# Add and RMS norm on one core: loops run to the last but one tile, and GpSimd itself waits for the last stores

## The chip, the cores and the metric

The kernel runs on one core of a Trainium2 chip. The metric is the device time of one execution in microseconds (us). The spread of the kernel before over several chips and sessions was 3725.68 to 3726.74 us. The engines are named as in the profile: DVE is VectorE, ACT is ScalarE, POOL is GpSimd, SP is SyncE; a trailing q (SPq, DVEq) marks the engine's sequencer, under which the traces list waits, branches, register operations and DMA issues.

## The reference

```python
batch, seq, dim = 32, 2048, 2048          # float32; gamma is all ones, eps 1e-6
z = x + residual
rms = np.sqrt(np.mean(z ** 2, axis=-1, keepdims=True) + eps)
return (z / rms * gamma).astype(np.float32)
```

There are 65,536 rows of 8 KB. Two inputs are read and one output is written once, 1610.7 MB in all.

## The kernel before

Each of the 128 partitions takes up to seven rows at a time, so a full tile is 128 x 7 x 2048 floats. There are 74 tiles, 0 to 73 (`last` is 73). SyncE issues every transfer. VectorE adds the residual, ScalarE squares and sums and takes the root, VectorE inverts and scales. Two z buffers alternate. The last tile comes in four pieces and has code of its own.

```python
last = n_tiles - 1                       # 73
LO = 3
n_iter = (last - 1 - LO) // 2            # 34
HI = LO + 2 * n_iter                     # 71
...
def sp_turn(sp, t):
    i = t.i
    t.wait(sp, "done", -1)               # the tile before is scaled
    # store of tile i - 1
    ...
    t.wait(sp, "add_a")
    load_r(sp, t, 1)                     # residual of tile i + 1
    t.wait(sp, "s_out", -1)              # the store has landed: its z is free
    # load of x of tile i + 1 (in four pieces where that is the last)
...
def sync_program(sp):
    ...
    for i in range(1, n_tiles):
        sp_turn(sp, Turn(i))
    for k, (a, b) in enumerate(tail):    # (0,2), (2,4), (4,6), (6,7)
        sp.wait_ge(tail_ev["done"], k + 1)
        sp.dma_start(out=rows(o_f, last)[:, a:b, :], in_=z[last % 2][:, a:b, :]
                     ).then_inc(s_tail, U)
    sp.wait_ge(s_tail, U * len(tail))
    sp.wait_ge(ev["s_out"][(last - 1) % 2], ((last - 1) // 2 + 1) * U)
    sp.sem_inc(fin, 1)
...
def vector_program(v):                   # scalar_program has the same shape
    ...
    for i in range(LO):
        dve_turn(v, Turn(i), lambda i, h: (2 * i + h + 1) * U)
    with v.Fori(0, 2 * n_iter, 2) as it:
        for i in range(LO, LO + 2):
            dve_turn(v, Turn(i, it), lambda i, h: it * (2 * U) + (2 * i + h + 1) * U)
    for i in range(HI, last):            # tiles 71 and 72, written out
        dve_turn(v, Turn(i), lambda i, h: (2 * i + h + 1) * U)
    # ... the last tile
...
nc.gpsimd.wait_ge(fin, 1)
nc.gpsimd.sem_clear(range(ids[0], ids[-1] + 1))
```

Inside a loop the threshold of each wait depends on the pass and is computed in a register (476 register operations on ScalarE's L209 in the trace of before, 14 in each of 34 passes); in a written-out turn it is a constant.

Of the kernel before, what the change touches and what calls it, by code (L numbers as in the profile page):

```python
# [9 lines left out]
def kernel(  # L10
# [17 lines left out]
    nc = tc.nc  # L28
# [12 lines left out]
    U = 16  # L41
# [8 lines left out]
    last = n_tiles - 1  # L50

    LO = 3
    n_iter = (last - 1 - LO) // 2
    HI = LO + 2 * n_iter
    assert n_iter >= 1

    def rows(t, i):
        k = sizes[i]
        return t[starts[i] : starts[i] + P * k, :].rearrange("(p r) m -> p r m", r=k)
# [11 lines left out]
    def sem(name):  # L71
        sems.append(ctx.enter_context(nc.semaphore(name)))
        return sems[-1]
# [17 lines left out]
    ev = {k: [sem(f"{k}{p}") for p in range(2)] for k in names}  # L91
# [4 lines left out]
    s_tail = sem("s_tail")  # L96
    fin = sem("fin")
# [3 lines left out]
    tail = [(0, 2), (2, 4), (4, 6), (6, 7)]  # L101
# [30 lines left out]
    def load_x(sp, t, d=0):  # L132
        i = t.i + d
        inc(sp.dma_start(out=z[i % 2][:, : sizes[i], :], in_=rows(x_f, i)), "x_in", i)

    def load_r(sp, t, d=0):
        i = t.i + d
        e = entry(i)
        inc(
            sp.dma_start(out=r_area[:, e : e + sizes[i], :], in_=rows(r_f, i)),  # L140
            "r_in",
            i,
        )

    def sp_turn(sp, t):
        i = t.i
        t.wait(sp, "done", -1)
        inc(
            sp.dma_start(out=rows(o_f, i - 1), in_=z[(i - 1) % 2][:, : sizes[i - 1], :]),
            "s_out",  # L150
            i - 1,
        )
        if i == last:
            return
        t.wait(sp, "add_a")
        load_r(sp, t, 1)
        t.wait(sp, "s_out", -1)
        if i + 1 == last:
            for k, (a, b) in enumerate(tail):
                sp.dma_start(  # L160
                    out=z[last % 2][:, a:b, :], in_=rows(x_f, last)[:, a:b, :]
                ).then_inc(x_tail[k], U)
        else:
            load_x(sp, t, 1)
# [84 lines left out]
    def sync_program(sp):  # L249
        load_x(sp, Turn(0))  # L250
        load_r(sp, Turn(0))

        sp.wait_ge(tail_ev["add"], 1)
        for q in range(4):
            sp.dma_start(  # L255
                out=stage[32 * q : 32 * q + 1],
                in_=gamma.partition_broadcast(1).rearrange("p (a b) -> p a b", a=16),
            ).then_inc(g_in, U)
        load_r(sp, Turn(1))
        load_x(sp, Turn(1))  # L260
        for i in range(1, n_tiles):
            sp_turn(sp, Turn(i))
        for k, (a, b) in enumerate(tail):
            sp.wait_ge(tail_ev["done"], k + 1)
            sp.dma_start(
                out=rows(o_f, last)[:, a:b, :], in_=z[last % 2][:, a:b, :]
            ).then_inc(s_tail, U)
        sp.wait_ge(s_tail, U * len(tail))
        sp.wait_ge(ev["s_out"][(last - 1) % 2], ((last - 1) // 2 + 1) * U)
        sp.sem_inc(fin, 1)  # L270

    def vector_program(v):
        v.memset(eps_tile[:, :], float(eps))  # L273
# [28 lines left out]
    def scalar_program(s):  # L302
# [13 lines left out]
        for k, (a, b) in enumerate(tail):  # L316
# [4 lines left out]
            ).then_inc(tail_ev["rms"], 1)  # L321

    sync_program(nc.sync)
    vector_program(nc.vector)
    scalar_program(nc.scalar)


    nc.gpsimd.wait_ge(fin, 1)
    ids = [a.num for a in sems]
    assert ids == list(range(ids[0], ids[0] + len(ids)))  # L330
    nc.gpsimd.sem_clear(range(ids[0], ids[-1] + 1))
# [35 lines left out]
```

## Time and profile before

| what | value |
|---|---|
| time, median of the first three runs | 3726.35 us (3725.92 to 3726.7) |
| span of the profiled run | 3724.7 us |
| VectorE, ScalarE busy | 62%, 29% |
| DMA share in each of 40 slices, and rate | 90% or more; mean 432 GB/s, steady 434 |
| instruction packets in the span | 4 |

The prediction below shows the lines of the page and of the waits. Two views that it only tells in words are these. The first is the list of DMA issues (transfer, engine, count, KB each, median us from issue to landing); the second the instructions of two lines at the end (count, shortest/median/longest duration in ns, first and last start in us):

```profile
out_dram<-z SPq DMA_DIRECT2D x71, 7168.0 KB, 34.5
```

```profile
L270 SPq EVENT_SEMAPHORE  x1: 28/28/28, 3723.5 to 3723.5; - x1
```

```profile
L331 POOLq EVENT_SEMAPHORE_RANGE_CLEAR  x1: 185/185/185, 3723.6 to 3723.6; - x1
```

A transfer is counted as landed when the last of its semaphore updates has arrived. A store takes 34.5 us to land with other transfers in flight: 7.34 MB alone at 434 GB/s would be 16.9 us (an estimate). The four instruction packets are of 8,192 bytes each in the trace, on a DMA queue of their own (q14); a packet is read here as a block of an engine's program, and is called a page of code below. And the end is a chain of very short things: SyncE sees the last store landed, tells GpSimd, and GpSimd clears the semaphores.

### The profile page before, as it was taken

What the parts mean: (1) busy time and instruction counts of PE and PEld (TensorE: products, weight loads), DVE (VectorE), ACT (ScalarE), POOL (GpSimd) and SP (SyncE); (2) the same over time, 40 slices, a digit from 0 to 9 for tenths busy, and PEclk for the clock granted to TensorE, in tenths of its full rate; (3) what the DMA queues carried; (4) which work ended last, traced back from release to release, by engine and by line L of the source; (5) the groups of instructions that cost most, each with busy time, mean ns of one, the idle gap of its engine ahead of it and who ended that gap; (6) DMA issues with size and microseconds to landing.
All of it is one profiled execution on the core that took longest, in us unless ns stands there. A gap on an engine that the chain in (4) does not pass through costs nothing.

```text
span 3724.7 us, 3652 instructions
## 1 busy us (share of the span) xinstructions
DVE 2302.5 (62%) x816; ACT 1072.4 (29%) x1176; POOL 0.2 (0%) x4
## 2 busy tenths in 40 slices
DVE  5666665566665566665566665566665566655566
ACT  2233322233322233322233322233322233322233
POOL 0000000000000000000000000000000000000000
DMA  9999999999999999999999999999999999999999
GB/s 420 432 434 434 434 434 434 432 434 434 435 434 434 434 434 436 434 434 434 433 434 434 434 434 434 434 434 434 434 434 434 434 434 434 434 434 434 434 434 398
DMA packets 32964, 1610.69 MB, mean 432 GB/s; under 512 B 3712, under 2 KB 3776, under 8 KB 3776
## 3 DMA queue, kind: packets, MB, share of 16 engines
q1 hardware_dynamic: 32960, 1610.66, 99.9%
q14 instruction: 4, 0.03, 0.0%
HBM read 1073.77 MB, written 536.87 MB: 432 GB/s over the span
## 4 chain that ended last, share of the span: by engine, by line
DMA 66%; DVE 22%; issue 9%; ACT 2%; SPq 0%; DVEq 0%; ACTq 0%
DMA out_dram<-z 33%; DMA z<-in_x_dram 33%; DVE z L170 15%; DVE z L175 7%; ACT sq_junk L221 1%; DMA r_area<-in_gamma_dram 0%; ACT rms L229 0%; DVE rstd L195 0%; DVEq L126 0%; SPq L255 0%; DVE r_area L274 0%; ACTq L209 0%; ACTq L126 0%; DVE tail_rstd L291 0%; SPq L160 0%
## 5 line engine op out<-in xcount | busy, mean ns | idle before, releaser
L170 DVE TENSOR_TENSOR z<-z,r_area 128x8192 f32<-128x8192 f32 (+2 forms) x150 | 1109.4, 7437 | 1253.2 <-DMA z<-in_x_dram 1227.6
L221 ACT ACTIVATE sq_junk<-z 128x2048 f32<-128x2048 f32 x512 | 963.4, 1882 | 2618.1 <-DVE z L170 2606.7
L175 DVE SCALAR_TENSOR_TENSOR z<-z,rstd,gamma_tile 128x2048 f32<-128x2048 f32 x505 | 1153.5, 2344 | 5.2
L195 DVE RECIPROCAL rstd<-rms 128x4 f32<-128x4 f32 (+2 forms) x146 | 25.3, 173 | 130.8 <-ACT rms L229 130.8
L221 ACT ACTIVATION_READ_ACCUMULATOR sq_junk<-z 128x1 f32 x512 | 95.4, 186 | 0.0
L229 ACT ACTIVATE rms<-ssq,eps_tile 128x4 f32<-128x4 f32 (+2 forms) x146 | 43.3, 297 | 13.4
L175 DVE SCALAR_TENSOR_TENSOR z<-z,tail_rstd,gamma_tile 128x2048 f32<-128x2048 f32 x7 | 16.2, 2346 | 0.1
L276 DVE LOAD_MASK_SELECT gamma_tile<-r_area x1 | 0.0, 14 | 16.4 <-DMA r_area<-in_gamma_dram 16.4
L276 DVE STREAM_SHUFFLE gamma_tile<-r_area 128x2048 f32<-128x2048 f32 x1 | 2.3, 2290 | 0.0
L274 DVE MEMSET r_area<- 128x2048 f32 x1 | 1.8, 1765 | 0.4 <-issue 0.4
L221 ACT ACT_TABLE_LOAD x1 | 1.3, 1283 | 0.9 <-SPq L75 0.9
L229 ACT ACT_TABLE_LOAD x1 | 1.3, 1283 | 0.1
L229 ACT ACTIVATE tail_rms<-tail_ssq,eps_tile 128x2 f32<-128x2 f32 (+1 forms) x4 | 1.2, 296 | 0.1
L273 DVE MEMSET eps_tile<- 128x1 f32 x1 | 0.1, 59 | 1.0 <-SPq L75 1.0
L291 DVE RECIPROCAL tail_rstd<-tail_rms 128x2 f32<-128x2 f32 (+1 forms) x4 | 0.6, 158 | 0.0
L348 POOL MEMSET const-bfloat16-1.0<- 128x1 bf16 x1 | 0.1, 102 | 0.0
L348 POOL MEMSET const-uint8-127<- 128x1 uint8 x1 | 0.1, 102 | 0.0
L348 POOL MEMSET const-float32-1.0<- 128x1 f32 x1 | 0.1, 99 | 0.0
L348 POOL MEMSET const-float32-0.0<- 128x1 f32 x1 | 0.1, 98 | 0.2 <-issue 0.2
## 6 DMA issues: line engine op xcount, KB each, us to landing
r_area<-in_residual_dram SPq DMA_DIRECT2D x72, 7168.0 KB, 27.2
z<-in_x_dram SPq DMA_DIRECT2D x71, 7168.0 KB, 33.8
out_dram<-z SPq DMA_DIRECT2D x71, 7168.0 KB, 34.5
z<-in_x_dram SPq DMA_DIRECT2D x3, 2048.0 KB, 26.3
out_dram<-z SPq DMA_DIRECT2D x3, 2048.0 KB, 13.9
r_area<-in_residual_dram SPq DMA_DIRECT2D x1, 5120.0 KB, 25.3
z<-in_x_dram SPq DMA_DIRECT2D x1, 5120.0 KB, 36.8
out_dram<-z SPq DMA_DIRECT2D x1, 5120.0 KB, 24.7
```

The costliest lines, as they stand in the source:

```text
L170: return v.tensor_add(out=s, in0=s, in1=r_area[:, e + a : e + b, :])
L175: ins = v.scalar_tensor_tensor(out=s, in0=s, scalar=rs[:, c + g - a : c + g - a + 1], in1=gamma_tile[:, :], op0=mult, op1=mult,)
L195: v.reciprocal(out=rstd[p][h][:, :n], in_=rms[p][h][:, :n]).then_inc(dve, U)
L221: s.activation(out=sq_junk[:, :], in_=src[:, g, :], func=Act.Square, accum_out=sq[:, g - a : g - a + 1],)
L229: return s.activation(out=rm, in_=sq[:, : b - a], func=Act.Sqrt, bias=eps_tile[:, :], scale=inv_d)
L273: v.memset(eps_tile[:, :], float(eps))
L274: v.memset(stage, 0.0).then_inc(tail_ev["add"], 1)
L276: v.stream_shuffle(gamma_tile[:, :].rearrange("p (a b) -> p a b", a=16), stage, [0] * 32)
L291: v.reciprocal(out=tail_rstd[:, a:b], in_=tail_rms[:, a:b]).then_inc(dve, U)
L348: nc = _bacc.Bacc("TRN2", target_bir_lowering=False, num_devices=1)
```

## The change

The intent is less code and one handshake less. Both loops go on to tile 72, so no written-out turn is left between loop and last tile; and GpSimd, which only has to know that all stores have landed, waits for their semaphores itself.

```diff
-    n_iter = (last - 1 - LO) // 2
+    n_iter = (last - LO) // 2
@@ sync_program
-        sp.wait_ge(s_tail, U * len(tail))
-        sp.wait_ge(ev["s_out"][(last - 1) % 2], ((last - 1) // 2 + 1) * U)
-        sp.sem_inc(fin, 1)
@@ end
-    nc.gpsimd.wait_ge(fin, 1)
+    nc.gpsimd.wait_ge(ev["s_out"][(last - 1) % 2], ((last - 1) // 2 + 1) * U)
+    nc.gpsimd.wait_ge(s_tail, U * len(tail))
```

## The prediction

> **What bounds the kernel now.** I read the page first, then the chain of waits in order of time, then the instructions in order of time round the last loop pass and the end. From the page:
>
> ```profile
> span 3724.7 us, 3652 instructions
> ...
> DVE 2302.5 (62%) x816; ACT 1072.4 (29%) x1176; POOL 0.2 (0%) x4
> ...
> DMA  9999999999999999999999999999999999999999
> ...
> DMA packets 32964, 1610.69 MB, mean 432 GB/s; under 512 B 3712, under 2 KB 3776, under 8 KB 3776
> ...
> DMA 66%; DVE 22%; issue 9%; ACT 2%; SPq 0%; DVEq 0%; ACTq 0%
> ```
>
> VectorE (DVE) is busy 62% of the span and ScalarE (ACT) 29%, while the DMA engines are at 90% or more in each of the forty slices. The work is two inputs and one output of 536.87 MB, 1610.69 MB in all; at the page's steady 434 GB/s that is 3711 us of a 3724.7 us span. So transfers bound it, and about 14 us is start and drain.
>
> The last row seems to say otherwise: the chain that ended last is a third compute. In order of time a full period of that chain reads: store 34.5 us, load of x 33.8, add 15.2, the wait for ScalarE 8.6, the scaling 9.1, and the next store: about 101.6 us for two tiles, because each of the two z buffers goes round once in two tiles. But two full tiles also move 6 transfers of 128 x 7 x 2048 x 4 bytes = 7.34 MB, which is 44.04 MB, and at 434 GB/s that is 101.5 us. The two agree since a landing time is stretched by the other transfers in flight; while the DMA row stays at 9, a shorter compute leg would be met by longer landings. The chain names the path, the DMA row the limit.
>
> [...] the trace has 50 to 69 ns for VectorE's loop branch and 40 to 50 ns for ScalarE's, so I use these. [...] The page of this trace has four instruction packets in the whole span (0.03 MB), and the DMA view from 3310 us to the end lists the data queue alone, although both loops leave at about 3561 us: here leaving the loop fetched nothing. [...]
>
> **The change, part by part.** There are 74 tiles, numbered 0 to 73. The loops start at tile 3 and take two tiles a pass.
>
> (1) The number of passes was (73 - 1 - 3) // 2 = 34, to tile 70, with tiles 71 and 72 written out after the loop; the trace has 34 loop branches on each engine. It becomes (73 - 3) // 2 = 35, to tile 72, and the written-out turns vanish. Adds, squares, roots, reciprocals, scalings and transfers stay: the same 816 and 1176 busy instructions. Two turns move into the loop form, where thresholds of waits are computed in registers. By the source view, divided by 34 passes, one ScalarE pass has 14 of them on L209 (476 in all), two on L126 and three on L306; 19 x 0.04 = 0.76 us of sequencer work at 35 to 50 ns each. One VectorE pass has eight (four on L196, one on L126, three on L279) of 40 to 69 ns, 8 x 0.05 = 0.40 us. These are for both tiles together, once.
>
> Do they lie on the path? The same four-row part of a turn, last loop pass first, then the written-out turn of tile 71, in order of time (start us, duration us):
>
> ```profile
> 3560.39 0.30 ACT L229 ACTIVATE rms<-ssq,eps_tile 128x4 f32<-128x4 f32 x1
> 3560.79 0.18 DVE L195 RECIPROCAL rstd<-rms 128x4 f32<-128x4 f32 x1 [1.70 <-ACT rms L229]
> 3561.00 9.12 DVE L175 SCALAR_TENSOR_TENSOR z<-z,rstd,gamma_tile 128x2048 f32<-128x2048 f32 x4
> 3570.15 0.34 SPq L149 DMA_DIRECT2D out_dram<-z  x1
> ```
>
> ```profile
> 3611.22 0.30 ACT L229 ACTIVATE rms<-ssq,eps_tile 128x4 f32<-128x4 f32 x1
> 3611.62 0.18 DVE L195 RECIPROCAL rstd<-rms 128x4 f32<-128x4 f32 x1 [1.70 <-ACT rms L229]
> 3611.83 9.12 DVE L175 SCALAR_TENSOR_TENSOR z<-z,rstd,gamma_tile 128x2048 f32<-128x2048 f32 x4
> 3620.98 0.34 SPq L149 DMA_DIRECT2D out_dram<-z  x1
> ```
>
> From root to store both take 9.76 us. The register operations run beside the instruction in progress (ScalarE's next threshold is ready 0.05 us into a 1.88 us square), so the loop form costs nothing measurable. Pass against pass it is the same: 101.65 us between stores 3417.65 and 3519.30 in the loop, 101.68 between 3519.30 and 3620.98, half of it written out. Term: 0.0 us, within 0.03.
>
> (2) Leaving the loop moves from 3561 to about 3663 us, next to the final tile. After tile 72's last scaling VectorE idles 5.62 us for the first piece of x, ScalarE 19.57 us for the first add of the final tile. A branch of 0.07 us, issued during the first scaling, [...] fits in. Term: 0.0 us.
>
> (3) The end. SyncE's own waits now:
>
> ```profile
> SPq L140 <- DVE z L170: 1689.2, 72, 24.6
> SPq L149 <- DVE z L175: 1190.8, 73, 32.6
> ...
> SPq L270 <- DMA out_dram<-z: 13.4, 1, 13.4
> ```
>
> The third row is the wait for the last stores: it ends at 3723.54 us, SyncE's increment of the handshake takes 0.03 us, and GpSimd's semaphore clear (L331, 185 ns) starts at 3723.60. The 13.4 us is landing time and stays; it only changes its engine. What goes is SyncE's instruction and the hop, 3723.597 - 3723.544 = 0.05 us. GpSimd gains a second wait; in this trace one instruction holds two waits (SyncE's did), so it costs nothing, or one further semaphore instruction of 0.02 us (the others on GpSimd are 17 ns) plus its turnaround, some 0.06 us. The other engines can pass the end's first handshake earlier, since SyncE signals after its last issue at 3710.1; but GpSimd's clear and what follows it still come after the landing, so at most another 0.1 us lies there. Term: -0.05 us, between +0.05 and -0.15.
>
> Sum: 0.0 + 0.0 - 0.05, so **3726.3 us** against 3726.35.
>
> **Rivals.** First, code size: fewer written-out turns might mean fewer instruction pages. Each packet is about 8 KB (0.03 MB over four), 0.02 us at 434 GB/s; even losing two gains under 0.1 us. Against it, the last loop exit could need a page it has not got. The four-packet count speaks against a stall in before; if a stall of 2 us came it would hide in the 5.62 us, and one that outlasted it by 2 us would give 3728. Second, register waits as a new limit: were the 0.76 and 0.40 us all exposed, 3727.5; the two equal 9.76 us stretches speak against it. Third, the drain: in the last 15 us the DMA share falls to half, and the window view by 2 us has 246, 82 and 29 GB/s from 3716 to 3722 us, so a few slow DMA engines finish last. A different arrangement of packets there could shift the end by a microsecond or two either way (3724.5 to 3728) with no instruction to blame. Nothing in the change touches the order of issues, so I take it as scatter. Fourth, GpSimd as a slower waiter: it must notice DMA increments itself, but its clear started within 0.03 us of SyncE's increment ending, so it is not slow.
>
> **Range and chances.** The effect is 0.05 us, the spread of the three runs 0.8 us (3725.92 to 3726.7), so the sign cannot be told. I widen for another session and for the drain: 3723.5 to 3729.5, a little more room above than below since a slow start or exit can only add. Two per cent is 74 us, more than any of the terms by a factor of thirty: same 0.98, faster 0.01, slower 0.01.
>
> **What would show it.** Right: the same busy counts (816 and 1176) and the same totals; 35 loop branches on VectorE and ScalarE, the last near 3663 us; 101.5 to 101.7 us between alternate stores to the end; root to store 9.76 us for tile 72; idle time before the first tail add still about 5.6 us and put down to the x load; no SyncE wait on the last store, and the clear on GpSimd within 0.1 us of the landing. Wrong: an idle stretch of VectorE after the last loop branch that no transfer explains, instruction packets near 3663 us, a drain from last issue to end that differs by over 1 us from 3724.7 - 3709.8 = 14.9 us, or a DMA row below 9 before the last slice.

Two things that it says beforehand are shown below: landings longer by what compute is shorter (38.7 us for 34.5 in e5), and the cost of a second wait on GpSimd (0.066 us from it to the clear in the changed kernel).

## The result, and the profile after

The changed kernel took 3726.32 us in the median of four runs (3726.25 to 3726.72), the kernel before 3726.47 us in four runs (3725.92 to 3726.7). The ratio is 1.0 with a 95% interval of 0.9983 to 1.0017. Ratios here are the mean time of one kernel's runs over that of the other's runs of the same rounds, so not quite the ratio of the medians.

The page of the changed kernel, in the lines that answer to those of before, and the instruction packets (queue: packets, MB, share):

```profile
span 3724.5 us, 3677 instructions
...
DVE 2302.6 (62%) x816; ACT 1072.4 (29%) x1176; POOL 0.2 (0%) x4
...
DMA  9999999999999999999999999999999999999999
...
q14 instruction: 4, 0.03, 0.0%
```

The work and the DMA row are the same, and so is the number of instruction packets. The 25 more instructions are those of one more loop pass: counted in the trace, 17 on ScalarE's sequencer and 8 on VectorE's, beside one fewer on SyncE and one more on GpSimd.

The loop branches of VectorE and of ScalarE (count, durations, first and last start):

```profile
L276 DVEq COMPARE_BRANCH  x35: 50/56/69, 207.2 to 3662.5; - x35
```

```profile
L303 ACTq COMPARE_BRANCH  x35: 40/45/50, 206.6 to 3661.9; - x35
```

There are 35, and the last is taken at about 3662 us, next to the last tile. What stands round that exit, in order of time (start us, duration us; in brackets the idle time before and what ended it), changed kernel first, then the one line of before that answers to its last:

```profile
3661.80 0.30 ACT L229 ACTIVATE rms<-ssq,eps_tile 128x4 f32<-128x4 f32 x1
3662.20 0.18 DVE L195 RECIPROCAL rstd<-rms 128x4 f32<-128x4 f32 x1 [1.70 <-ACT rms L229]
3662.41 9.12 DVE L175 SCALAR_TENSOR_TENSOR z<-z,rstd,gamma_tile 128x2048 f32<-128x2048 f32 x4
3671.56 0.34 SPq L149 DMA_DIRECT2D out_dram<-z  x1
...
3677.16 4.43 DVE L170 TENSOR_TENSOR z<-z,r_area 128x4096 f32<-128x4096 f32 x1 [5.63 <-DMA z<-in_x_dram]
```

```profile
3677.37 4.43 DVE L170 TENSOR_TENSOR z<-z,r_area 128x4096 f32<-128x4096 f32 x1 [5.62 <-DMA z<-in_x_dram]
```

From root to store tile 72 takes 3671.56 - 3661.80 = 9.76 us, as it did written out. VectorE then idles 5.63 us for the first piece of x, against 5.62: the exit has cost nothing that shows.

At the end, the waits of SyncE (us in total, times, longest), and the two lines of GpSimd:

```profile
SPq L149 <- DVE z L175: 1191.7, 73, 32.5
...
SPq L75 <- POOLq L75: 13.5, 1, 13.5
```

```profile
L325 POOLq EVENT_SEMAPHORE  x1: 17/17/17, 3723.4 to 3723.4; - x1
```

```profile
L328 POOLq EVENT_SEMAPHORE_RANGE_CLEAR  x1: 183/183/183, 3723.4 to 3723.4; - x1
```

SyncE's 13.4 us wait for the stores has gone from its list, and a wait of 13.5 us for GpSimd has come in its place: the end of the program holds SyncE until GpSimd has cleared. With the trace's own nanoseconds: before, the first instruction to be released by the landing starts at 3723.544 us and the span ends 1.125 us later; after, at 3723.381 us, and the span ends 1.125 us later. The ending is the same to the nanosecond that can be read. The hop saved (0.053 us from SyncE's instruction to the clear) is paid back by GpSimd's second wait, which got an instruction of its own (0.066 us from it to the clear). ScalarE and VectorE pass the closing handshake at 3710.0 us now and not at 3723.7 us, and nobody gains by it. The 0.2 us between the two spans is older than the change: the store of tile 67 was issued at 3417.65 us before and 3417.43 us after, where both kernels still run the same loop.

So the marks named beforehand are met, with one exception that both kernels share: from store to next but one store the changed kernel takes 101.65 to 101.67 us in its last passes, but 102.4 us across the page that SyncE fetches at about 3303 us (e12 says why). What is left to test is whether zero is the sum of zeros or of effects that cancel, and whether the reason given, transfers, is the reason.

### The profile page after: what moved, and what is told of

Read it like the earlier page. It is cut to its first block, busy times and chain, and to the rows that moved or that the text cites. A ratio compares the mean times of both kernels' runs of the same rounds, so it can differ in the third digit from the quotient of the medians.

```text
span 3724.5 us, 3677 instructions
## 1 busy us (share of the span) xinstructions
DVE 2302.6 (62%) x816; ACT 1072.4 (29%) x1176; POOL 0.2 (0%) x4
## 2 busy tenths in 40 slices
DMA packets 32964, 1610.69 MB, mean 432 GB/s; under 512 B 3712, under 2 KB 3776, under 8 KB 3776
## 4 chain that ended last, share of the span: by engine, by line
DMA 66%; DVE 22%; issue 10%; ACT 1%; SPq 0%; DVEq 0%; ACTq 0%
DMA out_dram<-z 33%; DMA z<-in_x_dram 33%; DVE z L170 15%; DVE z L175 7%; ACT sq_junk L221 1%; DMA r_area<-in_gamma_dram 0%; ACT rms L229 0%; DVE rstd L195 0%; DVEq L126 0%; SPq L255 0%; DVE r_area L271 0%; ACTq L209 0%; ACTq L126 0%; DVE tail_rstd L288 0%; SPq L160 0%
## 5 line engine op out<-in xcount | busy, mean ns | idle before, releaser
L229 ACT ACTIVATE rms<-ssq,eps_tile 128x4 f32<-128x4 f32 (+2 forms) x146 | 43.3, 297 | 13.4
## 6 DMA issues: line engine op xcount, KB each, us to landing
z<-in_x_dram SPq DMA_DIRECT2D x71, 7168.0 KB, 33.8
```

The costliest lines, as they stand in the source:

```text
L229: return s.activation(out=rm, in_=sq[:, : b - a], func=Act.Sqrt, bias=eps_tile[:, :], scale=inv_d)
```

## The experiments

| run | median us (range), timed runs | before in the same session | difference of medians |
|---|---|---|---|
| e1 loop part only | 3726.32 (3726.17 to 3726.71), 5 | 3726.43 | -0.11 |
| e2 ending only | 3726.47 (3726.27 to 3726.93), 5 | 3726.43 | +0.04 |
| e3 loops of one pass | 3729.07 (3728.73 to 3729.66), 4 | 3726.43 | +2.64 |
| e4 forty further hops | 3728.48 (3728.3 to 3728.93), 5 | 3726.43 | +2.05 |
| e5 short scaling | 3726.64 (3726.02 to 3726.84), 4 | 3726.39 | +0.25 |
| e6 longer VectorE turn | 3726.27 (3726.08 to 3726.56), 4 | 3726.39 | -0.12 |
| e7 fewer bytes | 3562.53 (3562.3 to 3562.74), 4 | 3726.39 | -163.86 |
| e8 long stall at the exit | 3726.42 (3726.35 to 3726.63), 5 | 3726.39 | +0.03 |
| e9 last store in 120 + 8 | 3727.33 (3727.16 to 3728.69), 5 | 3726.41 | +0.92 |
| e10 last store in 88 + 40 | 3728.09 (3727.93 to 3728.26), 5 | 3726.41 | +1.68 |
| e11 last two stores in 120 + 8 | 3732.89 (3732.47 to 3733.29), 5 | 3726.41 | +6.48 |
| e12 four pages of SyncE code | 3729.93 (3728.95 to 3730.5), 5 | 3726.3 | +3.63 |

All but e7 give the right result. Their 95% intervals of the ratio reach some 0.14% to each side, which is 5 us. Differences of 0.9 to 6.5 us are read here from ranges that do not overlap the range of before, and from the traces.

### The two parts alone (e1, e2)

e1 is the kernel before with only the `n_iter` line of the change; e2 is the kernel before with only the rest of it.

> Only the loop part of the change: 35 passes, the old handshake at the end. Main theory (transfers bound the kernel, the loop form and the late exit lie beside them): within 0.5 us of the kernel before. Rival (two effects that cancel: the loop form or the exit costs some tenths to 1.2 us, the new ending gives them back): 0.3 to 1.2 us slower than before.

> Only the ending of the change: 34 passes, GpSimd waits itself. Main theory: within 0.5 us of before; from the landing seen by the first waiting instruction to the end of the span the same 1.1 us as before, since the hop saved (0.05 us) is spent on GpSimd's second wait. Rival (cancelling effects): 0.3 to 1.2 us faster than before.

Each part alone is within 0.11 us of before, with overlapping ranges. Nothing cancels: both are zero. In e2's trace the time from GpSimd's first released wait (3723.363 us) to its clear is 0.066 us, as in the changed kernel.

### The loop form, multiplied (e3)

```diff
-    n_iter = (last - LO) // 2
+    n_iter = 1
```

> The changed kernel with its loops cut to one pass, so that 68 of the 70 tiles in the loops are written out. Main theory (register operations and branches run beside other work): within 1 us of before. Rival (the loop form's 0.76 us on ScalarE and 0.40 us on VectorE per pass lie on the path): 34 passes x 1.16 us = 39 us faster, 1 per cent. Second rival (written-out code has to be fetched and the fetches stall): slower by several us, with many more instruction packets than 4.

The rival of exposed register work would have given -39 us. It falls: there is no gain (one of a microsecond or two could be hidden under what made the run slower). But the main theory's "within 1 us" was wrong too: the run is 2.6 us **slower**, which is the second rival's sign. The page of e3 has the packets it named:

```profile
q14 instruction: 22, 0.18, 0.0%
```

Eighteen more instruction packets, 2.6 us more. VectorE shows no stall for them in the trace: the idle time before its scalings stays at 5.4 us in all against 5.2. How a fetch with no such stall costs time is the question of e12.

### The hop, multiplied (e4)

```diff
+        for k in range(20):                   # SyncE, after its waits for the stores
+            sp.sem_inc(fin, 1)
+            sp.wait_ge(back, k + 1)
         sp.sem_inc(fin, 1)
@@ GpSimd
+    for k in range(20):
+        nc.gpsimd.wait_ge(fin, k + 1)
+        nc.gpsimd.sem_inc(back, 1)
-    nc.gpsimd.wait_ge(fin, 1)
+    nc.gpsimd.wait_ge(fin, 21)
```

> The loop part of the change and the old ending, with 20 round trips between SyncE and GpSimd put ahead of the handshake: 40 further hops. If one hop costs 0.05 us, as the trace of before has it, 40 cost 2.1 us; with the turnaround of the wait instruction, up to 2.8 us. Rival (a hop's real cost is hidden in the landing, so it is near 0): under 0.5 us slower. Rival (a hop costs far more than its record, 0.2 us): 8 us slower.

Forty hops cost 2.05 us, 0.05 us each, and in the trace successive waits on GpSimd start 0.096 us apart, two hops with the turnaround of the waits. The handshake that the change removes is worth just that on the bare end of the program. It is too little to see in one kernel, and as shown above it was paid back.

### What bounds the steady part (e5, e6, e7)

The edits, shortened:

```diff
 e5:  -  v.scalar_tensor_tensor(out=s, in0=s, scalar=rs[...], in1=gamma_tile, op0=mult, op1=mult)
      +  v.tensor_scalar(out=s, in0=s, scalar1=rs[...], scalar2=None, op0=mult)
 e6:  +  if h == 0 and i > 0:               # between the adds and the first scaling
      +      for j in range(3):
      +          v.tensor_reduce(out=idle[:, j:j+1], in_=gamma_tile, op=add, axis=X)
 e7:  -  ...r_area[:, e : e + sizes[i], :]...
      +  k = sizes[i] - (4 < i < last)      # one residual row less in tiles 5 to 72
      +  ...r_area[:, e : e + k, :]...
```

> The changed kernel with the scaling by gamma left out (gamma is all ones here, so the result is still right): an instruction with one tensor input. If it takes half of 2.34 us, a tile's scaling of 7 rows is some 8 us shorter. Main theory (DMA engines bound the steady part): within 3 us of before, the landings longer by what the compute is shorter, the last tile's pieces perhaps a little earlier. Rival (the chain of store, load, add, square, scale bounds): the four-row scaling is on it once in two tiles, 36 x 4.6 us = 170 us faster; over all seven rows 300 us.

> The changed kernel with three sums over gamma, about 2.2 us each, put on VectorE between the adds and the scaling of every tile but the first and last: 6.6 us more per tile, VectorE busy some 75 per cent. Main theory: within 3 us of before, landings shorter by what the compute is longer. Rival (the chain bounds): 36 x 6.6 us = 238 us slower.

> The changed kernel with one row per partition less of residual loaded in each of tiles 5 to 72 (the result is wrong on purpose): 68 x 128 x 8192 bytes = 71.3 MB less. Main theory: at 434 GB/s that is 164 us faster, 4.4 per cent. Rival (the chain bounds, and only its own transfers count, which this load is not): within 20 us of before.

e5 takes 45% off the scaling, 7 x 1.06 = 7.4 us a tile, and e6 adds 480.9 / 72 = 6.7 us to each of 72 turns, and neither moves the time. The groups of the page (instruction, shapes, count, busy us, mean ns, idle before) with the store's row from the list of DMA issues, e5 first:

```profile
L175 DVE TENSOR_SCALAR z<-z,rstd 128x2048 f32<-128x2048 f32 x505 | 617.2, 1282 | 5.2
...
out_dram<-z SPq DMA_DIRECT2D x71, 7168.0 KB, 38.7
```

```profile
L197 DVE TENSOR_REDUCE idle<-gamma_tile 128x1 f32<-128x2048 f32 x216 | 480.9, 2282 | 0.0
...
out_dram<-z SPq DMA_DIRECT2D x71, 7168.0 KB, 29.7
```

Four scalings saved 4 x (2.344 - 1.282) = 4.2 us ahead of each store in e5, and the store takes 38.7 us where it took 34.5: 4.2 us longer. In e6 the store comes later and lands 4.8 us sooner after its issue. The chain of waits goes through compute, and between -7.4 and +6.7 us a tile it makes no difference what that compute costs: the landings take up what it leaves. e7 is the positive control: the changed kernel's own page with 71.3 MB less,

```profile
span 3561.0 us, 3677 instructions
...
DMA  9999999999999999999999999999999999999999
...
DMA packets 32964, 1539.39 MB, mean 432 GB/s; under 512 B 3712, under 2 KB 3776, under 8 KB 3776
```

is at the same rate, and 163.9 us shorter where 164 were expected. Bytes count; some 7 us of VectorE's work a tile, more or less, does not.

### The exit, made worse (e8)

```diff
         base = 2 * last * U                 # VectorE, between the loop and the last tile
+        for j in range(4):
+            v.tensor_reduce(out=idle[:, j:j+1], in_=gamma_tile, op=add, axis=X)
```

> The changed kernel with four sums over gamma, about 8.8 us, on VectorE between the loop and the last tile, as a long stall on leaving the loop. Main theory of the prediction: the 5.6 us that VectorE waits for x hide most of it, some 3 us stay on VectorE, and the last store is issued up to 3 us later. Then it depends on the drain: if one late DMA engine sets the end (it has work queued to the end), 0 to 0.7 us slower; if VectorE's chain sets it, 3 us slower; if nothing hides it, 8.8 us slower.

In order of time (VectorE's stall, its first add of the last tile, and the four last stores; start us, duration us):

```profile
3671.55 8.88 DVE L284 TENSOR_REDUCE idle<-gamma_tile 128x1 f32<-128x2048 f32 x4
...
3680.35 8.76 DVE L171 TENSOR_TENSOR z<-z,r_area 128x4096 f32<-128x4096 f32 x2
...
3694.16 18.76 SPq L266 DMA_DIRECT2D out_dram<-z  x4
```

Of 8.88 us the wait for x hides the larger part. The first add starts at 3680.35 us and not at 3677.16, and the last store is issued at 3712.59 us and not at 3709.59: 3.0 us later. Yet the kernel takes as long as before. The landing absorbed the 3.0 us, so VectorE's last stretch does not set the end either.

### The drain: one late DMA engine (e9, e10, e11)

In the trace every transfer raises its semaphore in 16 steps (3,712 updates for 232 transfers), as many as the page counts DMA engines; a step is read here as one engine's share that has landed. For the last store of the kernel before, the updates arrive at up to 3720.58 us for 15 engines and at 3723.53 us for the last. (One other update, at 3721.11 us, is that same engine's share of the piece before, 2.4 us earlier.) In its last 2.45 us that engine runs eight packets of 8 KB back to back, 0.306 us apart: it had a backlog. The last step of a landing trails the first by 1.06 us at the first load of x and by 6.65 us at the store of tile 72; why that grows between page fetches too is open. The attempt to beat both kernels was to give the late engine less.

```diff
-            sp.dma_start(out=rows(o_f, last)[:, a:b, :], in_=z[last % 2][:, a:b, :]
-            ).then_inc(s_tail, U)
+            for p, q in ([(0, 120), (120, 128)] if k == 3 else [(0, 128)]):
+                sp.dma_start(out=rows(o_f, last)[p:q, a:b, :], in_=z[last % 2][p:q, a:b, :]
+                ).then_inc(s_tail, U)
# e10: (0, 88), (88, 128);  e11: k >= 2;  GpSimd's count raised to match
```

> The changed kernel with the last store (one row per partition) cut into 120 and 8 partitions[...]. In the trace of before 15 of the 16 increments of that store are there at 3721.1 us and the last at 3723.5: one late engine. If the late engine is the sixteenth: 1.5 to 2.4 us faster. If it is another, or if the lateness is a completion latency and no backlog: within 0.5 us of before.

> As the run before it, cut into 88 and 40 partitions[...]. If the late engine is one of these five: 1.5 to 2.4 us faster; if it is among the lower eleven: up to 0.5 us slower[...].

> As the first, but both the third and the fourth piece of the last tile cut into 120 and 8 partitions. If the sixteenth engine is the late one, the next late engine sets the end, at about 3721 us plus its extra share: about as fast as with one piece, 1.5 to 2.6 us faster than before. If another is late: within 0.7 us, or a little slower.

All three miss, and are slower. The choice of the cuts rested on an assumption about which engines a store of fewer partitions uses; "the sixteenth" and "these five" are those that were meant to be spared, "the lower eleven" the others. No run shows it, so it is cut from the expectations of e9 and e10. In e9 the engine that lands last runs nine packets of the last store where it ran eight of the uncut one; in e10 it runs twelve. So neither of these cuts took work from it, and each gave it more; why, and which of the two pieces the further packets belong to, is not shown. In e9 a ninth packet (0.31 us) came, and one 16 KB packet just ahead of it took 1.0 us instead of 0.61; together 0.7 of the 0.9 us. In e10 four further packets (1.22 us) and a like slow one (0.40 us more) make 1.6 of the 1.7 us. In e11 the issues themselves became slow: the two issues for the fourth piece took 1.9 and 2.9 us where the uncut store's took 0.33. None of the three cuts made the end earlier, so no version was found that beats both kernels.

### What a page of code costs (e12)

Between the landings on either side of the page that SyncE fetches at about 3305 us, the gap between the last and the next to last increment grew by 0.75 to 0.78 us in the traces of before, after, e1, e2 and e4 (in e3 it did not grow, see below), though the packet's own record is 0.31 us. That ties the late engine to SyncE's fetches, and asks for a test that adds fetches and nothing else.

```diff
         else:
             load_x(sp, t, 1)
+        for _ in range(7):
+            sp.wait_ge(g_in, U)               # long since true
+            sp.sem_inc(fin, 1)
```

> The changed kernel with seven semaphore instructions that wait for nothing after the last transfer of each tile's turn on SyncE: 511 instructions more, four pages of 128, and nothing else. SyncE idles there, so as work they are hidden. In the traces of before, after and four experiments the page that SyncE fetches at about 3305 us lets the last increment of the transfers in flight arrive 0.76 us later against the next to last, all alike. If the page fetches delay the one late DMA engine that sets the end: four pages x 0.76 = 3.0 us slower (1.2 us if it is the 0.31 us of a packet's own record). If the fetches run on another engine than the late one: under 1 us. If nothing but busy engines counts: 0.

The trace has 504 instructions more (72 turns, not the 73 of the expectation). The page of the profile has four packets more than the changed kernel's, and the time is 3.6 us longer, where 3.0 was expected of a delayed late engine:

```profile
q14 instruction: 8, 0.07, 0.0%
```

That is 0.9 us a page on average, but the pages do not count alike. SyncE's last four, at 1677, 2305, 2951 and 3613 us, each make the last increment of the next landing 0.72 to 0.77 us later, and within two tiles after each an interval between stores is 0.7 us longer than the usual 50.8. Its page at 1018 us moves an increment that is not the last, by 0.8 us, and the last one stays. So does the one at 1137 us in the changed kernel, whose page at 3302 us is its only one to delay the last increment. Three further delays stand for 2.3 of the 3.6 us; the rest is open.

The seven instructions of each turn took idle time themselves: SyncE's wait for the scaling (the L149 row) is 1153.9 us in all where it was 1191.7. The end of the span in windows (window: length, busy DVE, ACT, POOL, granted clock, DMA share, GB/s), the kernel before and then e12:

```profile
3716.00:3720.00 4.00, 0.00 (x0) 0.00 (x0) 0.00 (x0) 1.00 0.39 164
3720.00:3724.60 4.60, 0.00 (x0) 0.00 (x0) 0.00 (x0) 1.00 0.04 18
```

```profile
3720.00:3724.00 4.00, 0.00 (x0) 0.00 (x0) 0.00 (x0) 1.00 0.17 74
3724.00:3728.00 4.00, 0.00 (x0) 0.00 (x0) 0.00 (x0) 1.00 0.04 16
```

Both end with one engine left: a share of 0.04 over some four microseconds is about the 1/16 = 0.06 of one engine that stops before the window does. In e12 the last landing comes 3.6 us later than in the changed kernel, and the last store is issued 3.6 us later too (3713.24 us against 3709.59), which fits loads that are complete only when the late engine has its share.

The trace of e3 has the same effect, with other late engines. Its 18 further pages (0.15 us each on average) are VectorE's and ScalarE's; whose page it is follows from counting the instructions that each engine has run, one page per 128 (in the trace of before SyncE had run 79 instructions at one of its two pages and 207 at the other). VectorE's six pages at 1076, 1559, 2031, 2489, 2947 and 3415 us each make the last increment 0.8 to 1.0 us later. In the list of the longest pieces of the chain (start us, us) they stand out, against stores of some 34.5 us and loads of some 33.8:

```profile
1079.85 35.35 DMA out_dram<-z
1588.41 35.18 DMA out_dram<-z
2029.66 34.80 DMA z<-in_x_dram
2503.79 35.35 DMA out_dram<-z
2945.22 34.79 DMA z<-in_x_dram
3419.71 35.16 DMA out_dram<-z
```

ScalarE's pages from 1727 us on move the last but one increment, by 0.5 to 0.7 us, and SyncE's at 3307 us the one before that, by 0.7 us; the last stays where it is. So, as far as the increments tell, the pages of the three engines go through three different DMA engines, and a page costs time where its DMA engine is the one that lands last. Why six delays of 0.8 to 1.0 us make the run only 2.6 us longer is open.

## Why the prediction was right

Point by point:

- **What bounds it.** Right, and shown: e5 and e6 moved VectorE's work by -7.4 and +6.7 us a tile without effect, e7 moved bytes and got 163.9 of 164 us.
- **Term 1, the loop form: 0.0 within 0.03 us.** Right. e1 is 0.11 us away with overlapping ranges, and removing 34 passes of register work (e3) brought nothing like 39 us. The size per pass was 17 operations net on ScalarE, where 19 were counted beforehand; it matters nothing.
- **Term 2, the exit: 0.0.** Right. The wait before the last tile is 5.63 us against 5.62, no page was fetched there, and a stall of 8.88 us (e8) left the time where it was. The prediction was too careful here: it gave 3728 for a stall that outlasts the idle time by 2 us; e8's outlasted it by 3 us and took 3726.42.
- **Term 3, the ending: -0.05 us.** Right in its range and off in its size: 1.125 us from landing to end in both kernels, so 0.00. The hop is 0.05 us as worked out (e4), but the hope that GpSimd's clear would carry both waits failed; the second became an instruction and took as much back. The further 0.1 us allowed for engines that pass the handshake sooner was not there.
- **The rivals.** The second, exposed register waits, falls with e3. The fourth, GpSimd as a slow waiter, falls with e2. The third, the drain as scatter, was half right: its length did not change (14.9 us from last issue to end in both), but it is not scatter, it is one engine's backlog, the same in every trace. The first, code size, had the one wrong size of the prediction: a page was put at 0.02 us, its bytes at the full rate, and one page of SyncE's code delays its DMA engine by about 0.75 us and costs 0.9 us on average (e12). The forecast survived since the change kept the packets at four, and that was luck: the prediction argued that a fetch would hide, not that there would be none more or less.
- **The number.** That 3726.3 us met 3726.32 so closely is luck too: four runs of the changed kernel spread over 0.47 us. And the five legs named for the chain's period add up to 101.2 us, not the 101.6 given; the rest of the measured period is the reciprocal and the short gaps between the legs.

## What to carry to other kernels

In this kernel, with the DMA row full from end to end, the chain of waits still runs through compute, but its landings stretch and shrink to fit (38.7 us in e5 and 29.7 in e6 for 34.5); test what bounds a kernel by moving bytes and compute separately, not by the shares of the chain. This change, which only rearranges waits and code beside full transfers, could gain no more than the hop at the very end, about 0.05 us, and even that was spent by the instruction that replaced it. Count instruction packets when loops are unrolled or an engine's program grows: in this kernel, held by its transfers, a page made the last step of a landing 0.7 to 1.0 us later (e3, e12) where it fell on the DMA engine that was last anyway, and four pages of SyncE's cost 0.9 us each on average.
